# Layer 0 of a fused transformer kernel: modulation and the k and v sums by quarters of the features instead of halves, weights of v loaded later

## The chip, the cores and the metric

The kernel runs on one core of a Trainium2 chip. The metric is the device time in microseconds of one execution. The kernel before took 2399.53 us (median of three runs, 2398.6 to 2400.83). The execution that was profiled took 2408.4 us, of which 2406.5 us lie between its first and its last instruction (its span); times inside the kernel are counted from the start of that span.

## The reference, cut to what matters

The program is a stack of four attention-like layers on 256 latent and 256 context tokens of 1024 features, followed by a second block with a mixture of experts. Only the start of the first layer is changed:

```python
def modulation(cvec, w_ada, b_ada):
    return jnp.split(jax.nn.silu(cvec) @ w_ada + b_ada, 3, axis=-1)
...
        sh_l, sc_l, gt_l = modulation(c, w_ada, b_ada)
        sh_c, sc_c, gt_c = modulation(c_ctx, w_ada, b_ada)
        h_l = rmsnorm(x_lat, g_pre) * (1.0 + sc_l[:, None, :]) + sh_l[:, None, :]
        h_c = rmsnorm(x_ctx, g_pre) * (1.0 + sc_c) + sh_c
        y_l, y_c = mixer(h_l, h_c, need_ctx=need_ctx)
...
    q_l, k_l, v_l, z_l = jnp.split(h_lat @ w_in, cuts, axis=-1)
```

The shift `sh` and the scale `sc` are each 1024 numbers per condition vector; both come out of the first 2048 columns of `w_ada`, a matrix of 1024 x 3072 floats. Each of the 1024 features of `h` needs its own shift and scale, and k and v are sums over all 1024 features.

## The kernel before

Everything is float32. A product with weights is done in three passes on values that are split in a high and a low part (`two_parts`, L108: the high part on ACT, L110, the rest on DVE, L111; `wsplit`, L113, does it for a loaded weight tile; `mm3`, L124, issues the three products). The products of the modulation are plain float32, and the trace counts two MATMUL records for each of them.

When the kernel is built, a scheduler puts the instructions of the whole program in one list for each engine. Each engine runs its list in order and waits on semaphores where the list says so; the DMA queue that SP issues is such a list too. Loads of weights go through `load` (L100), which takes one of six buffers of 128 x 1024 floats (512 KB); a load can be issued when the buffer six loads back has been read.

Layer 0 starts in `first_layer` (L439), called by `layer_a` (L508):

- `tokens` (L445) loads and normalises four blocks of 128 tokens, transposes them on PE in eight batches of four (L452) and copies them to `xT`.
- The weights of v (`wv`, two loads, called by `w_v()`) are requested and split next, then the first half of the modulation, then the weights of k (`wk`, two loads).
- `modulation` (L456) works out shift and scale of one half of the features: eight loads of `l0_w_ada`, each 128 partitions with two pieces of 512 floats (shift and scale of eight rows of the matrix are spread over the partitions), and for each load two products of 32 rows x 512 columns. The four groups of 32 PSUM rows of the tile `ada` hold shift and scale of even loads (rows 0 to 63) and of odd loads (rows 64 to 127). The sum gets the bias (`plus`, L233 to L235), four transposes turn it (L469), and five small DVE instructions (L471 to L475) make the tiles `modB` (shift) and `modA` (scale).
- `modulated` (L477) applies them to the four blocks of 128 features of that half: half of the columns on DVE (L481), half on ACT (L482), then a split into `hT` (L110, L111).
- The loop over the two halves issues `modulated`, then the modulation of the other half, then for each block k of 128 features nine products of 128 x 256 for three of the four token blocks of v (PSUM tiles `s`, `s`, `o`) and six of 128 x 512 for k (PSUM tiles `mm`). The fourth token block of v (PSUM tile `t`, 24 products) comes last.

After that PE starts with the queries (`mm<-hT,wp`, 48 products for q and z of the first head pair), while DVE rotates the keys (`rope`, L427 to L432) and splits them; the first logits (`s<-ks,qs`) need the keys and the queries.

Of the kernel before, what the change touches and what calls it, by code (L numbers as in the profile page):

```python
# [9 lines left out]
F32 = mybir.dt.float32  # L10
# [4 lines left out]
ALU = mybir.AluOpType  # L15
# [36 lines left out]
def tile_model(ctx: ExitStack, tc: tile.TileContext, A, out):  # L52
    nc = tc.nc
    V, S, G, T = nc.vector, nc.scalar, nc.gpsimd, nc.tensor
# [5 lines left out]
    def right(name, bufs):  # L60
        return ph1.enter_context(tc.tile_pool(name=name, bufs=bufs, side="right"))
# [4 lines left out]
    tmp = right("tmp", 2)  # L66
# [13 lines left out]
    ident = cb[:, 0:128]  # L80
# [13 lines left out]
    def smc(name, i=0, n=None):  # L94
        o, w = SM[name]
        return sm[:, o + i:o + (w if n is None else i + n)]
# [3 lines left out]
    def load(src, shape):  # L100
        t = raw.tile([128, 1024], F32, name="w", tag="w")
        v = t[:, 0:int(np.prod(shape))]
        if len(shape) == 2:
            v = v.rearrange("p (a b) -> p a b", b=shape[1])
        loaded[0] = nc.sync.dma_start(v, src)
        return v

    def two_parts(hi, lo, src):  # L108

        S.activation(hi, src, AF.Copy)  # L110
        V.tensor_tensor(lo, src, hi, op=ALU.subtract)  # L111
# [18 lines left out]
    def psum(tag, shape=(512,), rows=128, bufs=None):  # L130
        if len(shape) == 1:
            return ps.tile([rows, shape[0]], F32, name=tag, tag=tag, bufs=bufs)
        return ps.tile([rows, *shape], F32, name=tag, tag=tag, bufs=bufs)

    def mm(o, l, r, start=True, stop=True):
        return T.matmul(o, l, r, start=start, stop=stop)  # L136

    def evac(o, i):

        cnt[0] += 1  # L140
        if cnt[0] % 2:
            S.activation(o, i, AF.Copy)
        else:
            V.tensor_copy(o, i)  # L144
# [13 lines left out]
    scT = cst1.tile([128, 2, 8, 32], F32, name="scT")  # L158
# [74 lines left out]
    def plus(p, brow, keep):  # L233
        m = mpool.tile([128, 512], F32, name="modg", tag="modg", bufs=2) if keep else tmp.tile([128, 512], F32, name="mod", tag="th")
        V.tensor_tensor(m, p, brow, op=ALU.add)  # L235
        return m

    def row(src):
        r = tmp.tile([128, 512], F32, name="rows", tag="rows", bufs=2)
        nc.sync.dma_start(r, src)  # L240
        return r
# [51 lines left out]
    def new_hT(n):  # L293

        hs = [hpool.tile([128, 4, 512], F32R, name="hT", tag="w") for _ in range(4 if n == 512 else 2)]
        if n == 256:
            return [[u[:, :, 256 * j:256 * j + 256] for u in hs] for j in range(2)]
        return hs[0:2], hs[2:4]
# [140 lines left out]
    def first_layer(lp, w_v, w_k):  # L439

        hT = new_hT(512)
        xT = [lp.tile([128, 2, 512], F32, name="xT", tag=tag, bufs=2) for tag in ("pT", "pT", "qs", "qs")]
        a, b = [mpool.tile([128, 8, 2], F32, name="mod" + c, tag="mod" + c, bufs=2) for c in "AB"]

        def tokens(t):  # L445
            nc.sync.dma_start(x[t], A["xin"][t])
            xn = normalised(t, hT)
            for hh in range(2):
                p = psum("t", (4, 128))
                for q in range(4):  # L450
                    k = hh * 4 + q
                    T.transpose(p[:, q, :], xn[:, k * 128:(k + 1) * 128], ident)  # L452
                for q in range(2):
                    evac(xT[2 * hh + q][:, :, t * 128:(t + 1) * 128], p[:, 2 * q:2 * q + 2])

        def modulation(hh):  # L456

            brow = row(A["rows0"][hh])
            p = psum("ada", bufs=1)
            wv = A["l0_w_ada"][:, 0:2048].rearrange("(p k) (b c) -> p k b c", k=8, b=2)  # L460
            for k in range(8):
                ch = load(wv[:, k, :, 512 * hh:512 * hh + 512], (2, 512))
                for j in range(2):
                    g = j + 2 * (k % 2)
                    mm(p[32 * g:32 * g + 32, :], scT[:, 0, k, :], ch[:, j, :], k < 2, k >= 6)
            m = plus(p, brow, False)
            p = psum("ada", (4, 128), bufs=1)
            for q in range(4):
                T.transpose(p[:, q, :], m[:, q * 128:(q + 1) * 128], ident)  # L469
            ks = slice(4 * hh, 4 * hh + 4)  # L470
            V.tensor_copy(b[:, ks], p[:, :, 0:2])  # L471
            V.tensor_tensor(b[:, ks], b[:, ks], p[:, :, 64:66], op=ALU.add)
            V.tensor_scalar(a[:, ks], p[:, :, 32:34], 1.0, None, ALU.add)
            V.tensor_tensor(a[:, ks], a[:, ks], p[:, :, 96:98], op=ALU.add)
            V.tensor_tensor(a[:, ks], a[:, ks], smc("gpre0")[:, ks].unsqueeze(2).to_broadcast([128, 4, 2]), op=ALU.mult)  # L475

        def modulated(hh):  # L477
            for k in range(4 * hh, 4 * hh + 4):
                f = tmp.tile([128, 512], F32, name="hf", tag="th")
                src = xT[k // 2][:, k % 2]  # L480
                V.tensor_scalar(f[:, 0:256], src[:, 0:256], a[:, k, 0:1], b[:, k, 0:1], ALU.mult, ALU.add)  # L481
                S.activation(f[:, 256:512], src[:, 256:512], AF.Identity, scale=a[:, k, 1:2], bias=b[:, k, 1:2])  # L482
                two_parts(hT[0][hh][:, k % 4], hT[1][hh][:, k % 4], f)

        for t in range(4):
            tokens(t)
        pv = [psum("s", (256,)), psum("s", (256,)), psum("o", (256,), bufs=1)]
        pk = [psum("mm") for _ in range(2)]
        wv = w_v()
        modulation(0)  # L490
        wk = w_k()
        for hh in range(2):
            modulated(hh)
            if not hh:
                modulation(1)
            for k in range(4 * hh, 4 * hh + 4):
                hk = [u[hh][:, k % 4] for u in hT]
                for t in range(3):
                    mm3(pv[t], [u[:, t * 128:(t + 1) * 128] for u in hk], [u[:, k % 4, :] for u in wv[hh]], k == 0, k == 7)
                for m in range(2):  # L500
                    mm3(pk[m], [u[:, k, :] for u in wk[m]], hk, k == 0, k == 7)
        pv.append(psum("t", (256,)))
        proj_t(pv[3], 3, wv, hT)
        begin_mods(0)
        begin_mods(1)
        return hT, pk, pv
# [1581 lines left out]
def _layout(inp):  # L2088
    f = np.float32
    inp = {k: np.asarray(v) for k, v in inp.items()}  # L2090
    d = dict(_consts())
# [37 lines left out]
    for i in range(4):  # L2129
        b = inp[f"l{i}_b_ada"].reshape(6, 512)  # L2130
# [8 lines left out]
    rows0 = np.zeros((2, 128, 512), f)  # L2139
# [2 lines left out]
            rows0[hh, [j, 32 + j]] = inp["l0_b_ada"].reshape(6, 512)[[hh, 2 + hh]]  # L2142
    d["rows0"] = rows0

    def blocks(w, width):

        n = w.shape[1] // width
        return np.ascontiguousarray(w.reshape(8, 128, n, width).transpose(2, 1, 0, 3))
# [36 lines left out]
    b = inp["b_ada_2"][0].reshape(12, 512)  # L2185
# [40 lines left out]
```

## Time and profile before

| | |
|---|---|
| median of three runs | 2399.53 us |
| the profiled execution | 2408.4 us |
| its span | 2406.5 us |
| PE busy in the span | 2226.5 us, 93% |
| DVE busy, ACT busy | 1188.2 us (49%), 725.9 us (30%) |
| mean granted TensorE clock | 0.96 of full speed |
| moved by DMA | 576.71 MB, 240 GB/s on average |

The profile is read in stages, because the shares are means over stages with different limits. The change lies in the first 70 us. Matmul records end when their pipeline is empty, so the time that a product takes among others is the distance of two starts, not the length of a record.

### The profile page before, as it was taken

To read this page: it belongs to the slowest core of one execution; us is meant where nothing else is said; L and a number is where in the kernel's file an instruction comes from. 1 tells how busy PE (TensorE), PEld (TensorE's weight loads), DVE (VectorE), ACT (ScalarE), POOL (GpSimd) and SP (SyncE) were. 2 spreads that over 40 slices of the span, in tenths; PEclk is the share of its full clock that TensorE was granted. 3 is DMA by queue.
4 is the path that set the end of the run, shared out by engine and by line. 5 is a ranking of instruction groups with operands and counts; after the bars stand their busy time and mean duration, and the time that the engine had idled before them with its cause. 6 is when DMAs were issued, how large, how long until landed. Compare 5 with 4: busy or idle time off the path is not lost. (4 is left out here: it accounts for less than half of the span.)

```text
span 2406.5 us, 32540 instructions
## 1 busy us (share of the span) xinstructions
PE 2226.5 (93%) x12516; PEld 1372.9 (57%) x12516; DVE 1188.2 (49%) x2545; ACT 725.9 (30%) x1588; POOL 79.8 (3%) x125
## 2 busy tenths in 40 slices
PE   7999999999999999998998899989989899999997
PEld 4767777777788887677864343333334333334342
DVE  3877666656666669867544123232323333322332
ACT  3555454345333456554232011010111110101101
POOL 0000010000000010002200000000000000000000
PEclk9999999999999999999999899999989989999998
DMA  8443432333333245646237978787999868999995
GB/s 305 132 149 127 136 119 78 98 125 125 115 102 122 80 127 180 206 162 249 80 111 305 371 312 351 281 350 278 413 414 415 333 257 354 378 413 413 413 377 230
DMA packets 124828, 576.71 MB, mean 240 GB/s; under 512 B 11953, under 2 KB 12721, under 8 KB 91762
## 3 DMA queue, kind: packets, MB, share of 16 engines
q1 hardware_dynamic: 124530, 572.71, 62.5%
q8 instruction: 190, 3.11, 0.5%
q14 instruction: 108, 0.88, 0.1%
HBM read 571.61 MB, written 1.05 MB: 238 GB/s over the span
## 5 line engine op out<-in xcount | busy, mean ns | idle before, releaser
L136 PE MATMUL hg<-w,xq 128*64 128x512 f32 x2048 | 500.2, 621 | 15.2 <-PEq L1899 6.7
L136 PE MATMUL mm<-hT,wp 128*128 128x256 f32 (+1 forms) x1776 | 351.2, 342 | 0.6 <-DVE aqk L144 0.5
L136 PEld LDWEIGHTS hg<-w,xq 128*64 128x64 f32 x2048 | 161.1, 143 | 323.3 <-issue 306.3
L136 PEld LDWEIGHTS mm<-hT,wp 128*128 128x128 f32 x1776 | 272.5, 190 | 54.2 <-issue 19.8
L1729 DVE TENSOR_SCALAR gm<-hg 128x512 f32<-128x512 f32 (+1 forms) x37 | 25.6, 691 | 436.2 <-PE hg L136 434.6
L1748 PE MATMUL py<-w,aT 128*64 128x512 f32 x992 | 221.3, 592 | 1.1 <-DMA w<-w 1.0
L111 DVE TENSOR_TENSOR wp<-w,wp 128x1024 fp32r<-128x1024 f32 (+2 forms) x149 | 178.7, 1204 | 75.5 <-ACT wp L110 72.1
L136 PE MATMUL mm<-wp,hT 128*128 128x256 f32 (+1 forms) x1584 | 198.1, 284 | 5.1 <-DVE mixT L419 3.0
L136 PEld LDWEIGHTS mm<-wp,hT 128*128 128x128 f32 x1584 | 191.0, 191 | 11.0 <-DVE mixT L419 3.2
L110 ACT ACTIVATE wp<-w 128x1024 fp32r<-128x1024 f32 (+2 forms) x149 | 153.8, 1035 | 101.3 <-PE mm L136 55.2
L1730 ACT ACTIVATE um<-gm 128x512 f32<-128x512 f32 x32 | 20.2, 630 | 528.8 <-DVE gm L1729 528.8
L1748 PEld LDWEIGHTS py<-w,aT 128*64 128x64 f32 x992 | 84.3, 137 | 131.0 <-issue 118.9
L110 ACT ACTIVATE yeh<-gm 64x512 fp32r<-64x512 f32 x62 | 39.0, 628 | 202.3 <-DVE gm L1872 202.1
L1872 DVE SCALAR_TENSOR_TENSOR gm<-py,gsq,g 64x512 f32<-64x512 f32 x62 | 46.5, 750 | 100.1 <-PE py L1748 99.1
L136 PE MATMUL ada<-w,scT 128*32 128x512 f32 x576 | 83.6, 625 | 5.8 <-DMA w<-l_w_ada 5.7
L136 PEld LDWEIGHTS g<-P,xc 128*128 128x128 f32 x496 | 57.8, 191 | 24.8 <-issue 24.8
L136 PE MATMUL g<-P,xc 128*128 128x128 f32 x496 | 63.8, 281 | 1.1 <-DVE P L1678 1.1
L136 PE MATMUL hg<-w,xs 128*32 128x512 f32 x480 | 60.0, 650 | 5.0 <-DVE xs L144 3.8
L136 PE MATMUL s<-wp,oz 128*128 128x512 f32 x264 | 64.1, 392 | 0.0
L1766 DVE TENSOR_TENSOR xl<-xl,py 128x512 f32<-128x512 f32 x60 | 39.7, 686 | 41.8 <-PE py L136 38.2
L136 PEld LDWEIGHTS s<-wp,oz 128*128 128x128 f32 x264 | 49.1, 188 | 13.3 <-issue 2.5
L587 ACT ACTIVATE e<-e,nm 128x512 f32<-128x512 f32 x64 | 45.7, 716 | 30.9 <-DVE nm L586 30.7
(606 smaller groups left out, 3039.6 us busy)
## 6 DMA issues: line engine op xcount, KB each, us to landing
w<-w SPq DMA_DIRECT2D x383, 1024.0 KB, 15.5
w<-l_w_ada SPq DMA_DIRECT2D x96, 512.0 KB, 4.3
w<-w_ada SPq DMA_DIRECT2D x48, 512.0 KB, 4.4
w<-l_w_z SPq DMA_DIRECT2D x32, 512.0 KB, 4.6
w<-l_w_out SPq DMA_DIRECT2D x32, 512.0 KB, 4.2
w<-l_w_q SPq DMA_DIRECT2D x16, 512.0 KB, 5.3
w<-l_w_v SPq DMA_DIRECT2D x12, 512.0 KB, 5.0
w<-w_dqkv SPq DMA_DIRECT2D x12, 512.0 KB, 4.4
```

Of the source, the lines that this page charges most:

```text
L110: S.activation(hi, src, AF.Copy)
L111: V.tensor_tensor(lo, src, hi, op=ALU.subtract)
L136: return T.matmul(o, l, r, start=start, stop=stop)
L587: S.activation(e, e, AF.Exp, scale=0.125, bias=nm[:, c:c + 1], accum_out=den[:, c:c + 1])
L1729: V.tensor_scalar(gm, gate, 7.0, None, ALU.min)
L1730: S.activation(um, gm, AF.Sigmoid, scale=1.702)
L1748: i = T.matmul(p[64 * hh:64 * hh + 64, :], aT[:, kk % 4, 64 * (kk // 4):64 * (kk // 4) + 64], w2_tile(e, kk, hh), start=kk == 0, stop=kk == 7)
L1766: V.tensor_tensor(y[:, t, sl], y[:, t, sl], py, op=ALU.add)
L1872: V.scalar_tensor_tensor(w, p, gs, g2, ALU.mult, ALU.mult)
```

## The change

The modulation is worked out in four quarters of 256 features instead of two halves of 512. A new array `l0_w_mod` holds the same 2048 columns of `l0_w_ada`, laid out by quarters so that a load of 512 KB brings 4 KB in one piece to each partition: shift and scale of two eighths of the contraction. There are four loads for a quarter, sixteen in all, as before. For each load there are now four products of 32 rows x 256 columns, one for each group of 32 PSUM rows. A quarter is turned by two transposes instead of four, and the five small DVE instructions run on half the columns, four times instead of twice. `modulated` runs over two feature blocks at a time, and the loop over k and v issues the next quarter after each. The weights of v are requested after the first quarter of the modulation instead of ahead of it. The old columns of `l0_w_ada` beyond 2048 are used as before.

```diff
@@ -453,29 +453,32 @@
                 for q in range(2):
                     evac(xT[2 * hh + q][:, :, t * 128:(t + 1) * 128], p[:, 2 * q:2 * q + 2])
 
-        def modulation(hh):
-
-            brow = row(A["rows0"][hh])
-            p = psum("ada", bufs=1)
-            wv = A["l0_w_ada"][:, 0:2048].rearrange("(p k) (b c) -> p k b c", k=8, b=2)
-            for k in range(8):
-                ch = load(wv[:, k, :, 512 * hh:512 * hh + 512], (2, 512))
-                for j in range(2):
-                    g = j + 2 * (k % 2)
-                    mm(p[32 * g:32 * g + 32, :], scT[:, 0, k, :], ch[:, j, :], k < 2, k >= 6)
-            m = plus(p, brow, False)
-            p = psum("ada", (4, 128), bufs=1)
-            for q in range(4):
-                T.transpose(p[:, q, :], m[:, q * 128:(q + 1) * 128], ident)
-            ks = slice(4 * hh, 4 * hh + 4)
+        brows = {}
+
+        def modulation(q):
+
+            if q % 2 == 0:
+                brows[q // 2] = row(A["rows0"][q // 2])
+            p = psum("ada", bufs=1)[:, 0:256]
+            for k in range(0, 8, 2):
+                ch = load(A["l0_w_mod"][q, :, 2 * k:2 * k + 4], (4, 256))
+                for g in range(4):
+                    mm(p[32 * g:32 * g + 32, :], scT[:, 0, k + g // 2, :], ch[:, g, :], k == 0, k == 6)
+            m = tmp.tile([128, 512], F32, name="mod", tag="th")[:, 0:256]
+            V.tensor_tensor(m, p, brows[q // 2][:, 256 * (q % 2):256 * (q % 2) + 256], op=ALU.add)
+            p = psum("ada", (4, 128), bufs=1)[:, 0:2]
+            for u in range(2):
+                T.transpose(p[:, u, :], m[:, u * 128:(u + 1) * 128], ident)
+            ks = slice(2 * q, 2 * q + 2)
             V.tensor_copy(b[:, ks], p[:, :, 0:2])
             V.tensor_tensor(b[:, ks], b[:, ks], p[:, :, 64:66], op=ALU.add)
             V.tensor_scalar(a[:, ks], p[:, :, 32:34], 1.0, None, ALU.add)
             V.tensor_tensor(a[:, ks], a[:, ks], p[:, :, 96:98], op=ALU.add)
-            V.tensor_tensor(a[:, ks], a[:, ks], smc("gpre0")[:, ks].unsqueeze(2).to_broadcast([128, 4, 2]), op=ALU.mult)
-
-        def modulated(hh):
-            for k in range(4 * hh, 4 * hh + 4):
+            V.tensor_tensor(a[:, ks], a[:, ks], smc("gpre0")[:, ks].unsqueeze(2).to_broadcast([128, 2, 2]), op=ALU.mult)
+
+        def modulated(q):
+            hh = q // 2
+            for k in (2 * q, 2 * q + 1):
                 f = tmp.tile([128, 512], F32, name="hf", tag="th")
                 src = xT[k // 2][:, k % 2]
                 V.tensor_scalar(f[:, 0:256], src[:, 0:256], a[:, k, 0:1], b[:, k, 0:1], ALU.mult, ALU.add)
@@ -486,14 +489,14 @@
             tokens(t)
         pv = [psum("s", (256,)), psum("s", (256,)), psum("o", (256,), bufs=1)]
         pk = [psum("mm") for _ in range(2)]
-        wv = w_v()
         modulation(0)
-        wk = w_k()
-        for hh in range(2):
-            modulated(hh)
-            if not hh:
-                modulation(1)
-            for k in range(4 * hh, 4 * hh + 4):
+        wv, wk = w_v(), w_k()
+        for part in range(4):
+            hh = part // 2
+            modulated(part)
+            if part < 3:
+                modulation(part + 1)
+            for k in (2 * part, 2 * part + 1):
                 hk = [u[hh][:, k % 4] for u in hT]
                 for t in range(3):
                     mm3(pv[t], [u[:, t * 128:(t + 1) * 128] for u in hk], [u[:, k % 4, :] for u in wv[hh]], k == 0, k == 7)
@@ -2142,6 +2145,8 @@
             rows0[hh, [j, 32 + j]] = inp["l0_b_ada"].reshape(6, 512)[[hh, 2 + hh]]
     d["rows0"] = rows0
 
+    d["l0_w_mod"] = inp["l0_w_ada"][:, 0:2048].reshape(128, 8, 2, 4, 256).transpose(3, 0, 1, 2, 4).reshape(4, 128, 16, 256)
+
     def blocks(w, width):
 
         n = w.shape[1] // width
```

What the scheduler makes of it differs from before on SP, PE, DVE and ACT up to the first logits of layer 0; from there on each engine has the same instructions in the same order.

SP, the list of transfers from the first tokens to the tables after the modulation. `xl` and `xc` are the tokens, `w` is the ring of six weight buffers. Before:

```order
L446 DMA xl<-xin 128x1024 x2
L446 DMA xc<-xin 128x1024 x2
L105 DMA w<-l_w_v 128x1024 x2
L240 DMA rows<-rows 128x512
L105 DMA w<-l_w_ada 128x2x512 x8
L105 DMA w<-l_w_k 128x1024 x2
L240 DMA rows<-rows 128x512
L105 DMA w<-l_w_ada 128x2x512 x8
```

Now:

```order
L446 DMA xl<-xin 128x1024 x2
L446 DMA xc<-xin 128x1024 x2
L240 DMA rows<-rows 128x512
L105 DMA w<-l_w_mod 128x1024 x4
L105 DMA w<-l_w_v 128x1024 x2
L105 DMA w<-l_w_k 128x1024 x2
L105 DMA w<-l_w_mod 128x1024 x4
L240 DMA rows<-rows 128x512
L105 DMA w<-l_w_mod 128x1024 x8
```

Four loads of the modulation now stand ahead of the weights of v and k, and twelve behind them; before, eight stood between v and k.

DVE, from the last of the five small instructions of the first part of the modulation to the bias of the next part. `hf` is the modulated block, `hT` its low part, `wv` and `wp` the low parts of the weights of v and of k. Before:

```order
L475 TENSOR_TENSOR modA<-modA,sm 128x8
L481 TENSOR_SCALAR hf<-xT,modA,modB 128x256
L111 TENSOR_TENSOR wp<-w,wp 128x1024
L481 TENSOR_SCALAR hf<-xT,modA,modB 128x256
L111 TENSOR_TENSOR wp<-w,wp 128x1024
L111 TENSOR_TENSOR hT<-hf,hT 128x512 x2
L481 TENSOR_SCALAR hf<-xT,modA,modB 128x256 x2
L111 TENSOR_TENSOR hT<-hf,hT 128x512 x2
L235 TENSOR_TENSOR mod<-ada,rows 128x512
```

Now:

```order
L477 TENSOR_TENSOR modA<-modA,sm 128x4
L484 TENSOR_SCALAR hf<-xT,modA,modB 128x256
L111 TENSOR_TENSOR wv<-w,wv 128x1024
L484 TENSOR_SCALAR hf<-xT,modA,modB 128x256
L111 TENSOR_TENSOR wv<-w,wv 128x1024
L111 TENSOR_TENSOR hT<-hf,hT 128x512
L111 TENSOR_TENSOR wp<-w,wp 128x1024
L111 TENSOR_TENSOR hT<-hf,hT 128x512
L111 TENSOR_TENSOR wp<-w,wp 128x1024
L468 TENSOR_TENSOR mod<-ada,rows 128x256
```

The splits of the weights of v moved from the transposes of the tokens to here, so four weight splits instead of two stand between the first modulated blocks and the next part of the modulation.

PE, around the second part of the modulation. `ada` with `w` are the products of the modulation, `ada` with `mod` its transposes; `s`, `o` and `t` are the sums of v, `mm` those of k. Before:

```order
L136 MATMUL ada<-w,scT 32x512 x2
L136 MATMUL mm<-hT,wp 128x512 x4
L469 MATMUL ada<-cb,mod 128x128 x4
L136 MATMUL s<-wv,hT 128x256 x6
L136 MATMUL o<-wv,hT 128x256 x3
L136 MATMUL mm<-hT,wp 128x512 x6
L136 MATMUL t<-wv,hT 128x256 x3
```

Now, after the second of four parts:

```order
L136 MATMUL mm<-hT,wp 128x512 x5
L136 MATMUL ada<-w,scT 32x256 x4
L136 MATMUL mm<-hT,wp 128x512
L136 MATMUL t<-wv,hT 128x256 x4
L471 MATMUL ada<-cb,mod 128x128 x2
L136 MATMUL t<-wv,hT 128x256 x2
L136 MATMUL ada<-w,scT 32x256 x8
L136 MATMUL s<-wv,hT 128x256 x4
```

Behind the transposes PE now has two products of v and two loads' worth of the next part before it needs the modulated blocks of this part; before, it had a whole block of 15 products and three of `t`.

## Rows read from the trace of the kernel before

**Rows 1.** The page, busy us, share of the span and instructions by engine:

```profile
PE 2226.5 (93%) x12516; PEld 1372.9 (57%) x12516; DVE 1188.2 (49%) x2545; ACT 725.9 (30%) x1588; POOL 79.8 (3%) x125
```

**Rows 2.** Windows: from:to, length, busy per engine (instructions), clock, DMA share, GB/s:

```profile
27.00:32.40 5.40, 1.12 (x4) 0.72 (x4) 3.79 (x10) 3.65 (x6) 0.00 (x0) 0.50 1.03 387
32.40:37.00 4.60, 4.58 (x20) 2.37 (x22) 3.85 (x7) 2.73 (x5) 0.00 (x0) 0.59 1.02 353
37.00:49.00 12.00, 12.00 (x56) 5.38 (x53) 0.09 (x1) 0.00 (x0) 0.00 (x0) 1.00 0.69 260
49.00:65.20 16.20, 16.20 (x107) 14.66 (x107) 8.80 (x22) 8.61 (x16) 0.00 (x0) 1.00 0.50 180
```

**Rows 3.** Timeline of PE, 9 to 27 us: start, length, what, idle and releaser:

```profile
9.17 3.22 PE L452 MATMUL t<-cb,xn 128*128 128x128 f32 x12 [9.17 <-DVE xn L308]
16.14 1.92 PE L136 MATMUL ada<-w,scT 128*32 128x512 f32 x2
...
20.03 0.66 PE L452 MATMUL t<-cb,xn 128*128 128x128 f32 x4
20.62 1.92 PE L136 MATMUL ada<-w,scT 128*32 128x512 f32 x16
...
25.45 1.49 PE L136 MATMUL ada<-w,scT 128*32 128x512 f32 x4 [0.27 <-DMA w<-l_w_ada]
```

**Rows 4.** Timeline of ACT, the first split of a weight of v:

```profile
11.54 1.05 ACT L110 ACTIVATE wv<-w 128x1024 fp32r<-128x1024 f32 x1
```

**Rows 5.** Timeline of all engines, from the first half's bias to the first product:

```profile
26.97 0.69 DVE L235 TENSOR_TENSOR mod<-ada,rows 128x512 f32<-128x512 f32 x1 [5.41 <-PE ada L136]
...
27.72 1.12 PE L469 MATMUL ada<-cb,mod 128*128 128x128 f32 x4 [0.79 <-DVE mod L235]
...
29.81 1.09 ACT L482 ACTIVATE hf<-xT,modB,modA 128x256 f32<-128x256 f32 x2 [1.35 <-DVE modA L475]
30.07 1.22 DVE L111 TENSOR_TENSOR wp<-w,wp 128x1024 fp32r<-128x1024 f32 x1
...
32.42 0.80 PE L136 MATMUL s<-wv,hT 128*128 128x256 f32 x2 [3.58 <-ACT hT L110]
33.02 1.29 DVE L111 TENSOR_TENSOR hT<-hf,hT 128x512 fp32r<-128x512 f32 x2
```

**Rows 6.** Timeline of PE, products of the modulation among those of k and v:

```profile
33.15 1.94 PE L136 MATMUL ada<-w,scT 128*32 128x512 f32 x8
...
41.25 1.05 PE L136 MATMUL ada<-w,scT 128*32 128x512 f32 x4
42.23 0.39 PE L136 MATMUL o<-wv,hT 128*128 128x256 f32 x1
...
56.69 1.54 PE L136 MATMUL mm<-hT,wp 128*128 128x512 f32 x6
...
59.10 1.54 PE L136 MATMUL mm<-hT,wp 128*128 128x512 f32 x6
...
62.90 2.57 PE L136 MATMUL t<-wv,hT 128*128 128x256 f32 x21
```

**Rows 7.** Timeline of PE, second half: its transposes, and the first product behind them:

```profile
49.83 0.60 PE L469 MATMUL ada<-cb,mod 128*128 128x128 f32 x4
...
53.08 0.74 PE L136 MATMUL s<-wv,hT 128*128 128x256 f32 x4
```

**Rows 8.** Timeline of DVE and PE, from the keys to the first logits:

```profile
63.04 0.28 DVE L427 COPY ropeb<-kT 32x256 f32<-32x256 f32 x1 [1.23 <-ACT kT L142]
...
79.10 1.41 DVE L569 TENSOR_TENSOR qs<-qT,qs 64x512 fp32r<-64x512 f32 x2
79.84 1.20 PE L136 MATMUL s<-ks,qs 128*128 128x512 f32 x4 [0.87 <-DVE qs L569]
```

**Rows 9.** Windows of PE, two single microseconds: length, busy, clock, DMA share, GB/s:

```profile
26.00:27.00 1.00, 0.93 (x4) 0.50 1.09 401
...
36.00:37.00 1.00, 1.00 (x8) 0.92 0.99 279
```

## The prediction

> **What bounds the kernel now.** The page first: PE is busy 93% of the span [rows 1], so what counts is where PE waits. The windows by stage put the waits of the first 70 us ahead of 32.4 us: between 27 and 32.4 us PE works 1.12 us of 5.4, and from 37 us on it has no idle time up to 65.2 us [rows 2]. The timeline gives the cause: PE's last product of the first half of the modulation waits for its load and ends at 25.45 + 1.49 = 26.94 us [rows 3]; bias, four transposes, five small DVE steps, the modulated block and its split follow one by one, and the first product of v starts at 32.42 us [rows 5]. The transfers run at 387 GB/s meanwhile [rows 2], and ten loads of 512 KB (two for v, eight for the modulation) stand ahead of that point. So the stage has two parts: until 32.42 us a chain of loads and small steps ends last, after it PE itself.
>
> The sum is made against the profiled execution, 2408.4 us; the median of the runs is 2399.53 us, 8.9 us less, and I carry the difference found over to the median.
>
> **The change, part by part.**
>
> *First quarter of the modulation.* Four loads are enough now, and they take the places of the loads for v. The first of those had landed by 11.54 us [rows 4]; with the 256 KB of `rows` ahead and 0.524 MB / 387 GB/s = 1.35 us for each load, the fourth lands at about 16 us. PE isn't ready for it. Its list has 32 transposes and 16 products of the modulation, interleaved. [...] A lone 512-column product takes 1.92 us there [rows 3], one of 256 columns thus about 1.0 us. From 12.4 us (9.17 + 3.22): 1.0 for one product, 2.15 for eight transposes, 2 x 1.0 for the rest of load 1 and for load 2, 2.15 for eight transposes: 19.7 us. Then at full pace four pieces of about 0.5: the last product ends at 21.7 us, 5.2 us ahead of 26.94.
>
> How early the pace doubles is open. [...]
>
> *From there to the first product of v.* Before: 32.42 - 26.97 = 5.45 us [rows 5]. The bias has half the columns (0.69 us becomes about 0.42, an estimate from that row), two transposes instead of four (1.12 us becomes 0.56 at the lower pace); the small steps are bound by their start and stay. ACT splits one weight of v between the blocks where it split one of k. So 5.45 - 0.83 = 4.6, and the first product stands at 26.3 us, 6.1 us ahead.
>
> *What PE has to do from there until the sums of k are done* (62.90 us, where the last 21 products of `t` start [rows 6]). Before, 62.90 - 32.42 = 30.5 us:
> - eight blocks of nine and six products, one every 59.10 - 56.69 = 2.42 us: 19.4;
> - modulation [rows 6]: 1.9 us for the pair of loads at 33.15, six single loads at 42.23 - 41.25 = 0.98 plus about 0.2 for changing over (an estimate: the `o` product behind one has a record of 0.39 us, where the 21 of `t` stand 2.41 / 21 = 0.115 apart): 9.0 in all;
> - transposes 0.36, three products of `t` 0.35.
>
> That is 29.1; the other 1.4 us are the lower clock, 0.50 from 26 us until it rises in the 37th microsecond [rows 9], after 3 us of steady products.
>
> After:
> - the same 19.4, and 7 products of `t` (four move ahead of the end): 0.8;
> - twelve loads of the modulation in ten places. No row shows a 256-column product. From below: sixteen records (eight products, four loads) took 1.92 us when four groups of rows overlapped [rows 3], 0.48 us for two loads' groups at half the columns. From above: if the groups don't overlap better than the two of a single load did, 0.98. I take 0.55, nearest to the lower row, because now all four groups come with one load: 12 x 0.55 + 10 x 0.2 = 8.6;
> - three times two transposes: 1.05.
>
> Sum 29.85. To it come waits that weren't there:
> - *DVE in the first quarter.* Four weight splits of 1.22 us [rows 5] instead of two stand among the first blocks, because those of v left the stage of the transposes. The first modulated block stood 29.81 - 26.97 = 2.84 us behind the bias [rows 5], now 0.83 less: 21.7 + 2.0 = 23.7. From there DVE has block, split of v, block, then a wait for ACT (two blocks 1.09 [rows 5], second split 1.05 [rows 4]: until 25.9); then 1.2 + 0.65 + 1.2 + 0.65 + 1.2 = 30.8 us. Until then PE has 2.42 + 0.75 = 3.2 us of work, begun at 26.3, so it loses 30.8 - 29.5 = 1.3.
> - *The second quarter.* From the end of the transposes to the product that uses them: 53.08 - 50.43 = 2.65 us [rows 7]. PE has two products of `t` and two loads behind them, 0.25 + 1.3: it waits 1.1. In quarters three and four a block stands between (2.9 to 3.3 us of work): nothing.
> - *The lower clock.* Up to 30.8 us it is covered by DVE; beyond that between 0 and 1.4 us as before. I take 0.7.
>
> Together 29.85 + 3.1 = 33.0, so the sums of k are done at 59.3 us instead of 62.9: 3.6 us ahead.
>
> *Loads.* Six buffers now hold the weights of v and k until DVE has split them, so loads 7 to 11 of the modulation start only at 25 to 31 us. Three of them one behind the other take 3 x 1.35 = 4.1 us, and by the list above PE asks for each 3 to 8 us after it is free to start. I cost that at nothing: PE's own work on the blocks hides it, and if DVE fell 4 us behind, every further us would show. The loads of q and z queue behind these; the queries need them only after the sums. POOL's list isn't touched.
>
> *After the sums.* DVE is the bound from the first rotated key at 63.04 us to the split queries at 79.10, where PE waits 0.87 us for it [rows 8]. It does the same steps in that stretch, so the logits come ahead by what the sums of k came ahead; the four products of `t` that moved (0.46 us) are lost in that wait. From there the lists agree, so the gain stays: **3.5 us**, 2396.0 us by the median. That is 0.15%, inside the 0.2% (4.8 us) that a measurement of this kernel can tell from no change.
>
> **The rivals.**
>
> *The clock rises earlier at the start.* [...] Then three to four pieces of about 1.0 run in 0.5 each, the chain to the keys starts 1.7 us earlier, and PE keeps 1.1 to 2.2 us of that, as DVE's splits shift with it. Against: the early products are short and stand among transposes. It gives 2396.0 - 1.6 = 2394.4 us. Chance 0.2.
>
> *The clock stays low longer.* PE's start is spotty now: 1.3 us of waits by 30.8 us, 1.1 us in the second quarter. If it runs at 0.50 until 36 us as before, 5.2 us do the work of 2.6: 1.9 us more than I counted. If the waits of the second quarter let it fall once more, 1.5 more. 2398 to 2399.4 us. For: before, it was down from 26 us on [rows 9], after PE had waited for loads between short products. Against: from 30.8 us on PE is about as busy as it was before the rise at 36 us. Chance 0.23.
>
> *Four groups don't overlap (slower).* If a load costs 0.98 as a single load did [rows 6], twelve loads cost 12 x 0.43 = 5.2 us more, and the four at the start about 2.3 us: 3.5 turns into -4.0, 2403.5 us. It turns from gain to loss where a load costs 0.55 + 3.5/16 = 0.77 us. Against: the sixteen records in 1.92 us. Chance 0.07.
>
> **How the numbers follow.** The forecast, with 1.5 us to either side for the terms that I estimated, has 0.5. The range takes in the two clocks and reaches from 2391.8 to 2400.4 us: it leaves out most of the slower rival and about 0.1 at the fast end, where an early clock and short loads (0.48) come together. Faster by over 0.2% (below 2394.7 us): most of the early clock and the forecast's fast edge, 0.27. Slower by over 0.2% needs the third rival with the low clock as well: 0.04. Within: 0.69.
>
> **What would show it.** The last product of the first quarter near 21.7 us; first product of v near 26.3; on DVE four splits in a row up to 30.8 with PE waiting for them; starts of a load's products 0.5 to 0.6 us apart; an idle time of about 1 us ahead of the third pair of blocks; the queries starting near 59.3 + 17 x 0.115 = 61.3 us; the wait ahead of the first logits grown by 0.5 us. It is wrong if a load takes over 0.77 us, if the clock is low beyond 33 us, or if a later stage doesn't shift with the logits.

## The result and the profile after

The changed kernel takes 2373.63 us (median of 6 runs, 2365.69 to 2376.36), the kernel before 2400.34 us in the runs beside it (6 runs, 2398.6 to 2407.28). The ratio is 0.9879, 95% interval [0.9858, 0.9899]: about 27 us less, where 3.5 were forecast. The profiled execution takes 2374.81 us, with a span of 2373.0. That of before, at 2408.4 us, lies some 10 us over the medians of its kernel (2394.5 to 2400.3 in all comparisons here), so the two traces differ by 33.5 us, and not each difference between them is the change's.

The page's line of the engines, after (it answers [rows 1]):

```profile
PE 2209.1 (93%) x12580; PEld 1363.3 (57%) x12580; DVE 1189.4 (50%) x2557; ACT 726.2 (31%) x1588; POOL 80.3 (3%) x125
```

PE is busy 17.4 us less although it has 64 products more, and idle 16 us less (2373.0 - 2209.1 = 163.9 against 180.0). Where that lies is read stage by stage. First the stage that was changed: the timeline of PE after, to be laid beside [rows 3, 5, 6, 8]. Columns: start, length in us, what, and in brackets the idle time before it with its releaser.

```profile
9.03 3.23 PE L452 MATMUL t<-cb,xn 128*128 128x128 f32 x12 [9.03 <-DVE xn L308]
12.18 1.06 PE L136 MATMUL ada<-w,scT 128*32 128x256 f32 x2
13.17 1.93 PE L452 MATMUL t<-cb,xn 128*128 128x128 f32 x8
15.03 1.06 PE L136 MATMUL ada<-w,scT 128*32 128x256 f32 x14
16.03 1.09 PE L452 MATMUL t<-cb,xn 128*128 128x128 f32 x8
...
18.20 1.06 PE L136 MATMUL ada<-w,scT 128*32 128x256 f32 x14
...
23.81 1.22 PE L136 MATMUL s<-wv,hT 128*128 128x256 f32 x4 [3.56 <-ACT hT L110]
...
29.47 0.64 PE L136 MATMUL ada<-w,scT 128*32 128x256 f32 x8
30.04 0.97 PE L136 MATMUL s<-wv,hT 128*128 128x256 f32 x6
...
57.48 2.17 PE L136 MATMUL t<-wv,hT 128*128 128x256 f32 x17
59.49 11.36 PE L136 MATMUL mm<-hT,wp 128*128 128x512 f32 x48
...
74.34 1.18 PE L136 MATMUL s<-ks,qs 128*128 128x512 f32 x4 [1.20 <-DVE qs L572]
```

The first quarter is done at 18.20 + 1.06 = 19.26 us (before: the first half at 26.94), the first product of v starts at 23.81 instead of 32.42, the sums of k are done at 57.48 instead of 62.90, and the logits start at 74.34 instead of 79.84: 5.5 us ahead. Until here the change does what it says, 2 us better than forecast.

The rest comes much later. Between the first logits and some 115 us (times of before) a few instructions of the first layer's attention still stand in another order than before, so the lists agree later than the section on the change says. From there on PE, DVE, ACT and POOL run the same instructions in the same order. I matched DVE's instructions of the two traces one by one: the lead is 5.5 us at the first logits, 6.6 at 175 us, 11 at 1475, 32 at 1975. It grows most where the experts are worked out one after the other. Each expert copies its gate once to `gsq`; that copy serves as a mark. The answer for its line in the stretch of 1470 to 2010 us, before and after (count, shortest/median/longest ns, then the first and the last start):

```profile
L1707 DVE COPY gsq<-g x8: 150/150/150, 1491.4 to 2006.4; 128x2 f32<-128x2 f32 x8
```

```profile
L1710 DVE COPY gsq<-g x8: 150/150/152, 1480.3 to 1973.2; 128x2 f32<-128x2 f32 x8
```

In both it is the copies of the 4th to the 11th expert. The same seven experts take 515.0 us before and 492.9 us after: 22 us, in a stage that the diff doesn't touch. I call this the **expert stretch** below.

What PE waits for there, from 1000 us to the end (total, times, longest, us), first before, then after:

```profile
PE hg L136 <- PEq L1885: 10.2, 6, 6.2
PE hg L136 <- PEq L1899: 6.7, 10, 5.2
PE g L1739 <- PEq L1899: 5.5, 1, 5.5
...
PE hg L136 <- issue: 4.0, 3, 3.1
```

```profile
PE hg L136 <- PEq L1902: 6.5, 10, 5.0
PE g L1742 <- PEq L1902: 5.2, 1, 5.2
PE g L136 <- PEq L1888: 4.8, 1, 4.8
```

PEq is PE's own sequencer, and L1885 and L1899 (L1888 and L1902 after) are the two `tc.If(n > 64, ...)` around the work of an expert that more than 64 tokens chose. All rows of PEq and of issue together are 39.8 us before and 24.4 after; the largest waits for DVE and ACT are the same to 0.1 us (`gsq` 19.0, `yeh` 16.7). So the largest waits for data are not what changed. One such place in the timeline of PE, the end of the same expert, before:

```profile
1883.62 0.39 PE L136 MATMUL py<-yel,gTq 128*128 128x512 f32 x1
1885.37 0.50 PE L136 MATMUL py<-yeh,gTq 128*128 128x512 f32 x1 [1.36 <-ACT yeh L110]
1892.08 1.06 PE L136 MATMUL hg<-b1p,sel 96*64 96x512 bf16 x4 [6.21 <-PEq L1885]
```

and after:

```profile
1863.39 0.51 PE L136 MATMUL py<-yeh,gTq 128*128 128x512 f32 x1 [1.35 <-ACT yeh L110]
1864.04 0.62 PE L136 MATMUL hg<-b1p,sel 96*64 96x512 bf16 x4
1864.59 0.51 PE L136 MATMUL py<-yel,gTq 128*128 128x512 f32 x1
```

The same product waits 6.21 us before and not at all after. During that wait of before the DMA queues (1885.4 to 1892 us; packets, MB, share) show

```profile
q1 hardware_dynamic: 548, 2.69, 101.5%
q8 instruction: 1, 0.02, 1.0%
q14 instruction: 1, 0.01, 0.3%
```

a transfer of the instruction queue of 0.02 MB, while the weights of the experts fill the engines. In the whole trace this queue carries 190 such packets, 3.11 MB, so 16.4 KB each; I take them for code that comes in blocks. Between 100 and 1000 us, ahead of the experts, there are 42, one for some 251 of the 10561 products and weight loads that PE has there (after: 42, one for some 255 of 10697). One packet proves little, since in the expert stretch of before one comes every 9 us (58 in 515 us). But each of the eight waits of over 2 us on PEq or issue that PE has behind 1000 us in the trace of before holds one, inside it or in flight at its start.

### The profile page after: what moved, and what is told of

The parts are those of the page before. It is cut to its first block, busy times and chain, and to the rows that moved or that the text cites. A ratio compares the mean times of both kernels' runs of the same rounds, so it can differ in the third digit from the quotient of the medians.

```text
span 2373.0 us, 32692 instructions
## 1 busy us (share of the span) xinstructions
PE 2209.1 (93%) x12580; PEld 1363.3 (57%) x12580; DVE 1189.4 (50%) x2557; ACT 726.2 (31%) x1588; POOL 80.3 (3%) x125
## 5 line engine op out<-in xcount | busy, mean ns | idle before, releaser
L136 PE MATMUL hg<-w,xq 128*64 128x512 f32 x2048 | 492.5, 615 | 13.2 <-PEq L1902 6.5
L136 PE MATMUL ada<-w,scT 128*32 128x512 f32 (+1 forms) x640 | 79.2, 574 | 4.9 <-DMA w<-l_w_ada 3.9
L111 DVE TENSOR_TENSOR yel<-gm,yeh 64x512 fp32r<-64x512 f32 x60 | 41.2, 687 | 26.3 <-ACT yeh L110 25.4
## 6 DMA issues: line engine op xcount, KB each, us to landing
w<-w SPq DMA_DIRECT2D x383, 1024.0 KB, 16.4
```

## The experiments

Three theories. **A, position in time:** a lead of 5 us shifts where PE's gaps fall, and with them the spells at the lower clock. **B, carry:** later stages are lastingly faster by themselves, so a delay costs just itself. **C, place of the code:** the change makes PE's program longer by 130 instructions (64 products, 64 weight loads, 2 semaphore waits, counted in the traces) in front of everything later, so the ends of the code blocks fall elsewhere against the branches of the experts. Medians are compared within a job; before took 2394.48 us in the first, 2395.51 in the second, 2397.54 in the third.

**A delay of some 5.7 us, in the changed kernel and in the one before.** Both repeat the last products of v:

```
-        proj_t(pv[3], 3, wv, hT)
+        for r in range(3):
+            proj_t(pv[3], 3, wv, hT)
```

> The changed kernel, but the 24 products of the fourth token block of v are worked out three times (the first two results are thrown away). That adds 48 x 0.115 = 5.5 us to PE between the sums of k and the queries, of which up to 1.2 us go into the wait ahead of the first logits: the logits should stand at 78.6 to 79.9 us, within about 1 us of where they stand in the kernel before (79.84), and 4.3 to 5.5 us behind the changed kernel (74.34). Theory A, the gain behind the first layer hangs on where PE's idle gaps fall in time, and with that on the spells at the lower clock: the later work stands again where it stood before, so most of the 22 us are lost again, and the time lies at 2390 to 2405 us. Theory B, something in the changed kernel makes the later stages faster for good, whatever the hour: the delay is all that is added, 2373.6 + 4.3 to 5.5 = 2378 to 2379 us.

> The kernel before, with the same 48 products more at the same place: 5.5 us on PE, 0.9 us of them hidden by the wait ahead of the first logits, so the logits at 84 to 85 us. Theory A: the spells at the lower clock change their places, and the time moves by something else than the delay: below 2400 or above 2410 us. Theory B: 2400.3 + 4.6 = 2405 us, within 2 us.

e1: 2397.22 us, ratio 1.001 [0.9987, 1.0032], all of the gain gone. e2: 2388.57 us, ratio 0.998 [0.9958, 1.0001]: B's 4.6 us more lie outside that interval, which reaches from 10 us less to 0.2 us more. B falls with both. A stood, but explained nothing in advance: its bound for e2 (below 2400 us) holds for the kernel before in this job as well. The first product of the logits moved less than expected, to 76.50 us in e1 and 81.98 in e2, but at 175 us the whole delay is there (6.4 us in both, by the table below). Seen from C, each of these edits also adds 96 instructions to PE.

**The change's two parts.** e3 moves only the loads of v's weights behind the first modulation, by halves as before; e4 has the quarters, with v's weights loaded first as before.

```
-        wv = w_v()
         modulation(0)
-        wk = w_k()
+        wv, wk = w_v(), w_k()
```

```
+        wv = w_v()
         modulation(0)
-        wv, wk = w_v(), w_k()
+        wk = w_k()
```

(the second against the changed kernel)

> The kernel before, with nothing of the change but the place of the weights of v: their loads and splits stand behind the first half of the modulation (halves, old layout). The first half's last load comes two loads (2.7 us) sooner, but four splits of 1.22 us stand between the first blocks, so the sums of k should be done within 2 us of 62.9. Theory A: the time moves by more than the sums of k do, either way, by up to 20 us. Theory B, if the later gain comes from the order of the loads of v: it shows here, 2375 to 2382 us; if not, 2398 to 2402 us.

> The changed kernel, with the weights of v loaded and split ahead of the modulation as in the kernel before. The fourth load of the modulation comes two loads later than in the changed kernel, but only two splits stand between the first blocks: the first product of v at 25 to 27 us, the sums of k done at 57 to 60 us (62.9 before, 57.5 with the whole change). Theory A: the time is anywhere between 2365 and 2405 us, by the spells, and doesn't follow from the sums of k. Theory B, if the later gain comes from the quarters: 2373 to 2377 us.

e3: 2397.81 us, ratio 1.0008 [0.9985, 1.0031]; e4: 2376.72 us, 0.9909 [0.988, 0.9938]. The quarters carry the effect or most of it (18 us against the kernel before in this job, where the whole change has some 26 in others), the later loads alone none. In e4's trace the logits start at 73.08 us, sooner than with the whole change; in e3's at 81.19. PE's program is 2 instructions shorter in e3 and 130 longer in e4: this doesn't separate A from C.

**Only the code is moved.** PE has nothing to do until 9 us. There, ahead of the first transpose, stand products of one element on constants that are set at once:

```
     V.memset(scT, 0.0)
+    pz = psum("t", (4, 128))
+    for _ in range(32):
+        mm(pz[0:1, 0, 0:1], mhalf[:, 0:1], mhalf[:, 0:1])
```

e5 has them in the kernel before (128 instructions), e6 in the changed kernel (258 in all), e8 has 40 of them in e1's kernel (386), and e7 is the changed kernel once more.

> The kernel before with 32 products of a single element ahead of the first transpose, where TensorE waits for the first rows until 9.17 us anyway. No other work is moved in time; only TensorE's program gets longer by about as many instructions as the change adds to it (64 products and their 64 weight loads). Theory A (the gain behind the first layer hangs on where the work falls in time, by way of the clock): first logits and total unchanged, 2392 to 2397 us, and TensorE's waits on its own sequencer, on issue and on the branches of the expert stage (from 1000 us on) stay near 37 us. Theory C (the gain behind the first layer comes from where the boundaries of the code blocks that the instruction queue brings in fall against the branches of the expert stage): those waits fall to about 24 us as in the changed kernel, and the total is 2378 to 2384 us although the first layer gains nothing.

> The changed kernel with the same 32 products of one element at the start: TensorE's program is now some 258 instructions longer than before's, about one block of the instruction queue (16 KB), so that the block boundaries of the expert stage lie as in the kernel before. Theory A: 2372 to 2377 us, as the changed kernel, waits near 24 us. Theory C: the waits of the expert stage come back to about 37 us, and the total is 2386 to 2391 us: only the 5.5 us of the first layer and a little of the clock are left of the gain.

> The changed kernel itself, beside the others on one chip, and for a second profile of it. Both theories: 2371 to 2377 us; the logits 5 to 6 us sooner than before, and waits of the expert stage near 24 us again, at the same branches as in its first profile.

> The changed kernel with the delay of e1_after_delay (the last products of v three times) and 40 products of one element at the start, which bring TensorE's program from 226 to some 386 instructions over before's, that is one block more than the changed kernel's 130. Theory A: 2395 to 2399 us, as e1_after_delay, since the work falls at the same times. Theory C: the code lies as in the changed kernel, waits near 24 us, and the total is the changed kernel's and the delay of 5.7 us: 2376 to 2383 us.

In the trace of e5 they cost nothing, since the rows come later anyway:

```profile
0.92 1.74 PE L136 MATMUL t<-mhalf 128*1 128x1 f32 x64 [0.92 <-DVE mhalf L92]
9.11 3.23 PE L455 MATMUL t<-cb,xn 128*128 128x128 f32 x12 [6.45 <-DVE xn L311]
```

e5: 2386.31 us, ratio 0.9955 [0.9932, 0.9978], without any earlier logits worth naming (0.8 us). e6: 2396.78 us, 1.0002 [0.9977, 1.0026]: the changed kernel loses its gain to 32 products that nobody waits for. e7: 2369.84 us, 0.9899 [0.9865, 0.9934], 1 us under its range; its logits start at 75.00 us, 4.8 us ahead of before where the first profile has 5.5. e8: 2376.04 us, 0.991 [0.9879, 0.9942]: e1's kernel with 40 products more is 19.5 us below before, where e1 was 2.7 above. A says that e8 equals e1, e6 equals e7 and e5 equals before; it is wrong three times. In e5, PE, DVE and ACT run the instructions of before behind the new products in the same order, and in e6 those of the changed kernel (but for one pair on DVE), so that only the place of PE's code is different. The first and last mark of the expert stretch, in e6 and in e8:

```profile
L1713 DVE COPY gsq<-g x8: 148/148/150, 1476.0 to 1995.8; 128x2 f32<-128x2 f32 x8
```

```profile
L1714 DVE COPY gsq<-g x8: 147/148/149, 1485.6 to 1980.1; 128x2 f32<-128x2 f32 x8
```

519.8 us in e6, as before (515.0), and 494.5 in e8, as after. e6's program is 258 instructions longer than before's, e8's is 256 longer than the changed kernel's. Of e6's waits of over 2 us in the stretch, these are back, the last of them at the product shown above:

```profile
1521.40 0.39 PE L136 MATMUL py<-yeh,gTq 128*128 128x512 f32 x1 [3.43 <-issue]
...
1884.89 1.06 PE L136 MATMUL hg<-b1p,sel 96*64 96x512 bf16 x4 [5.71 <-PEq L1891]
```

C had the sign and the place, not each size: e6 lies 6 us over its range, e5 2 us, and e5's waits are 30.4 us, not 24.

**The changed kernel's place exactly, and other places.** e9 is e5 with one bf16 product more (two instructions, 130 in all); e10, e11 and e12 are the changed kernel with 16, 24 and 48 of the products of one element.

```
+    mbf = const.tile([128, 16], BF16, name="mbf")
+    V.memset(mbf, -0.5)
...
     for _ in range(32):
         mm(pz[0:1, 0, 0:1], mhalf[:, 0:1], mhalf[:, 0:1])
+    mm(pz[0:1, 0, 0:1], mbf[:, 0:1], mbf[:, 0:1])
```

> e5_before_shift with one more product (its weight load and its matrix instruction), so that TensorE's program of the kernel before is longer by 130 instructions, exactly as far as the changed kernel's, where e5's was by 128. Theory C (the places of the code blocks against the branches decide the gain behind the first layer): the stall of some 5 us between 1880 and 1900 us that e5 kept goes too, waits near 24 us, total 2375 to 2381 us, the changed kernel's and its 5 us in the first layer. A rival in which e5's missing part has nothing to do with the code: 2384 to 2389 us, as e5.

> The changed kernel with 16 products of one element at the start: TensorE's program 194 instructions over before's instead of 130, a quarter of a block on. Theory C: another set of stalls at the branches, so a total that may lie anywhere from the changed kernel's 2372 to 2391 us, and waits of the expert stage that go with it (each us of waits at least one us of time). Without an influence of the code: 2371 to 2377 us.

> The changed kernel with 24 products of one element at the start: 226 instructions over before's, the code layout of e1_after_delay without its delay of 5.7 us. Theory C: waits near 34 us at the same branches as in e1, total 2387 to 2394 us, that is e1's 2397 less the delay. Theory A (it was the delay that cost 24 us in e1): 2371 to 2377 us.

> The changed kernel with 48 products of one element at the start: 322 instructions over before's, 66 past a whole block. Theory C: not the changed kernel's layout, so again a total between 2372 and 2392 us with waits of the expert stage that go with it. Without an influence of the code: 2371 to 2377 us.

e9: 2377.2 us, ratio 0.992 [0.9899, 0.9941]. The kernel before, with its halves and its logits at the old time, has most of the changed kernel's gain, through 33 products that compute nothing. Its marks:

```profile
L1713 DVE COPY gsq<-g x8: 148/150/150, 1484.3 to 1978.9; 128x2 f32<-128x2 f32 x8
```

494.6 us, with no wait of over 2 us in the stretch. (The one that e5 kept there isn't at the product named above, as the expectation has it: it is 2.41 us on issue, at 1802 us.) The rival's 2384 to 2389 us are out. e10: 2379.37 us, 0.9935 [0.9911, 0.996]; e11: 2388.91 us, 0.9966 [0.9947, 0.9985], 8.6 below before in its job, where e1 was 2.7 above before in its own: 11 us apart where the delay is 5.7, and its waits are 39.0 us instead of 34; e12: 2394.34 us, 0.9991 [0.9971, 1.001], 2 us over its range.

All kernels in the order of their place in a block, which I take as 256 instructions (an estimate from the 251 and 255 above, and from e6 and e8): PE's instructions over before's; what is left of that after taking off 256; the expert stretch of the profiled run and all waits for PEq and issue from 1000 us on; the logits' region against before (median of DVE's instructions between 175 and 200 us); the time.

| kernel | longer by | place | stretch, us | waits, us | at 175 us | median, us |
|---|---|---|---|---|---|---|
| e1 | 226 | 226 | 503.6 | 33.5 | -0.2 | 2397.2 |
| e11 | 226 | 226 | 511.3 | 39.0 | -5.8 | 2388.9 |
| e3 | -2 | 254 | 511.5 | 38.5 | +0.2 | 2397.8 |
| before | 0 | 0 | 515.0 | 39.8 | 0 | 2394.5 to 2400.3 |
| e6 | 258 | 2 | 519.8 | 39.5 | -3.6 | 2396.8 |
| e12 | 322 | 66 | 510.5 | 37.1 | -4.6 | 2394.3 |
| e2 | 96 | 96 | 492.4 | 25.4 | +6.4 | 2388.6 |
| e5 | 128 | 128 | 496.3 | 30.4 | -1.4 | 2386.3 |
| e9 | 130 | 130 | 494.6 | 23.3 | +0.4 | 2377.2 |
| e8 | 386 | 130 | 494.5 | 24.2 | -1.1 | 2376.0 |
| e4 | 130 | 130 | 497.9 | 26.1 | -7.2 | 2376.7 |
| after, e7 | 130 | 130 | 492.9, 494.5 | 24.4, 23.1 | -6.6, -4.2 | 2373.6, 2369.8 |
| e10 | 194 | 194 | 504.7 | 33.9 | -7.2 | 2379.4 |

The five profiled runs at place 130 agree in stretch and waits whatever their first layer does; those around 0 agree as well. With 256 to 258 instructions more the stretch is nearly the same again: 515.0 us before and 519.8 in e6, 492.9 after and 494.5 in e8. Stretch and waits are each those of one execution, which for before lies 8 to 14 us above the median of its kernel, for e3 and e11 9 us. Nor do waits and medians go together one to one: e1 waits 6 us less than before and is no faster. What the traces and runs show is this: packets of 16.4 KB on the instruction queue, about one for 251 to 255 of PE's products and weight loads where no expert stands, a stretch that comes back after some 256 instructions, and waits of up to 6.21 us behind the `If`s. That such a wait is one for code is theory C's reading of these; no row shows it by itself.

## Why the prediction was wrong

**The step that failed is the last:** "From there the lists agree, so the gain stays". The lists do agree, from 115 us on, and the first layer's lead is still there at 175 us. But equal lists aren't equal programs: the same instructions lie 130 further on in PE's code, and the later stages moved by far more than the logits, where the prediction had them move together. Of some 26 us, e9 gives the part of the place alone: 2397.5 - 2377.2 = 20 us. The other 5 or so fit the 4.8 and 5.5 us by which the logits came sooner in the two traces of the changed kernel. Its ratio is 0.988 to 0.990 where e9's is 0.992, and e8, without most of the lead, takes 6.2 us more than e7 beside it (2376.0 and 2369.8). These differences are no larger than the intervals, so the medians alone don't show that part. The change makes the programs of DVE and ACT a little longer too (12 instructions more on DVE); no run moves those by themselves. That the four groups of a quarter add 32 products, each recorded as two, to PE's program was in front of me as a cost of 8.6 us and not as a length.

What the 20 us consist of can be read from the expert stretch, 515.0 us before and 494.6 in e9. PE's windows over it, from the first mark to the last, before and then e9 (length, busy with the count of products, clock, DMA share, GB/s):

```profile
1491.40:2006.40 515.00, 464.49 (x2444) 0.94 0.86 344
```

```profile
1484.30:1978.90 494.60, 457.08 (x2444) 0.97 0.88 359
```

PE runs the same 2444 products. In e9 it idles 13.0 us less (37.5 against 50.5), and its waits for PEq and issue there are 12.8 us less (5.8 against 18.6). It is busy 7.4 us less, at a granted clock of 0.97 instead of 0.94. The lower clock goes with the waits: the windows around the two longest waits of before in the stretch, and around the same products in e9, show

```profile
1783.00:1795.00 12.00, 8.90 (x27) 0.57 1.03 408
1885.00:1897.00 12.00, 5.42 (x12) 0.57 1.03 412
```

```profile
1770.80:1782.80 12.00, 12.00 (x53) 0.89 1.03 421
1867.20:1879.20 12.00, 11.43 (x42) 0.86 1.02 423
```

so PE loses the wait itself and works at the lower level around it (the clock records of before show 0.50 from 1783.8 to 1794.0 and from 1886.2 to 1896.4 us). Nothing else is left over: in all 14 profiled kernels PE's busy time in the stretch, less half of its part at the lower level, comes to 440 to 442 us (worked out from the clock records of the traces), so that idle time and clock are the whole difference between them there.

Over whole executions time and clock go together too: over all 30 runs of before in the first job the correlation of time and mean granted clock is -0.89, and the means of the runs are 0.965 to 0.966 for before, 0.970 for the changed kernel (6 runs), 0.971 for e9. But not every spell at the lower clock belongs to the place: that of before between 350 and 400 us (0.90 there, 1.00 after) is missing or shorter in every other profiled kernel, with the gain or without. Open is how two instructions of place make up e5's 9 us over e9: their stretches differ by 1.7 us, their waits by 7.1, and 3 of these lie behind the stretch.

Now the steps of the first layer.

- *The first quarter ends at 21.7 us.* It ended at 19.26, 2.4 us sooner. The rival of the early clock came true: twelve transposes at 9.03 us take 3.23 us and eight at 13.17 take 1.93, but the eight at 16.03, after the first products at 12.18 and 15.03, take 1.09. Before, the pace rose only behind the product at 16.14 [rows 3]: four transposes took 1.12 us at 17.99 and 0.66 at 20.03. For the slow part no run shows a level of the clock: the records of the granted clock begin at 14.9 us after and at 19.1 before, both with 1.00, about where the pace rises. The forecast's steps up to 19.7 us thus carry on the pace of [rows 3], and the four pieces of about 0.5 us at full pace behind them were my estimate; at 18.20 us 14 records of 256 columns took 1.06 us. The first record stands 2.7 us (after) and 3.0 us (before) behind the start of the first product of the modulation; two traces make no rule.
- *First product of v 4.6 us behind the bias.* 23.81 - 19.32 = 4.5: right, and so it stood 2.5 us ahead of the forecast.
- *PE waits 1.3 us for DVE's four splits.* Wrong. They stand at 21.46, 23.27, 25.01 and 26.75 us, the last done at 27.97, and PE has no wait between 23.81 and 35 us. The products of the next quarter's loads filled it, and at the lower clock PE's own work was longer. The windows after (length, busy of PE, PEld, DVE, ACT, POOL with counts, clock, DMA share, GB/s):

```profile
20.00:27.00 7.00, 3.44 (x13) 2.50 (x12) 6.31 (x13) 4.98 (x7) 0.00 (x0) 0.63 0.79 247
27.00:32.40 5.40, 5.40 (x40) 2.99 (x40) 0.97 (x1) 0.00 (x0) 0.00 (x0) 0.85 0.91 328
```

- *The lower clock beyond that, 0.7 us.* Too little, in return. The granted clock is 0.63 from 20 to 27 us, and its 0.85 from 27 to 32.4 us means (1 - 0.85) x 5.4 / 0.5 = 1.6 us at the lower level (0.50), so that it rose for good at some 28.6 us. PE's first 4.8 us behind 23.81 thus did the work of 2.4. The two errors nearly cancel: from the first product of v to the sums of k it was 57.48 - 23.81 = 33.7 us, where 33.0 were forecast.
- *0.55 us for a load's products.* 30.04 - 29.47 = 0.57: right, and the slower rival, which needed 0.77, is out.
- *1.1 us of waiting in the second quarter.* 0.78 us on the modulated block, and 0.52 us on issue a little ahead of it: right.
- *Loads cost nothing.* Right: from 19 to 60 us PE waits for no DMA.
- *Queries at 61.3 us, the wait ahead of the logits grown by 0.5.* 59.49, and 1.20 us against 0.87: the queries came with the quarter's 2 us, the wait grew by 0.33. DVE's chain shifted along as forecast.

So the first layer gave 5.5 us (4.8 in the second profile) in place of 3.5, and the term that was mis-sized is the pace at the start. The rival that had it gave 2394.4 us. No case that I wrote down held the 20 us.

## What to carry to other kernels

In a kernel with branches an edit changes one more number, the length of each engine's program ahead of them; here, for PE's, the same stretch took 492.4 to 519.8 us. After an edit, look for waits on the engine's own sequencer and on issue behind the branches, and compare kernels with the program padded to the same place (a few products of one element in a gap that is there anyway) before the edit is credited with the difference. Here the padded kernel before (2377 us) shows that some 20 of the 26 us are not the change's own; what is left for it, about 5 us, is no larger than the intervals. The padding, which cost nothing in an idle gap (1.74 us of work ahead of 9.11 us in e5), is worth a try of its own. A gain that appears far behind the edit, in a stage that the diff doesn't touch, is no carry until a kernel without the edit has been seen without it.

## What the runs showed of the hardware

- Behind an `If` PE waited up to 6.21 us on its own sequencer, with one 16.4 KB packet of the instruction queue inside the wait and the weights at 101.5% of the DMA engines (rows above). The same stretch of seven experts takes 492.4 to 519.8 us, by the place of the same instructions in the code. The effect repeats when PE's program grows by some 256 instructions (before 515.0 us and e6 519.8, after 492.9 and e8 494.5).
- Such a wait came with a lower clock as well: around the two longest in the expert stretch of before the granted clock was 0.57, around the same products without the wait 0.86 to 0.89.
- A place isn't just good or bad: between 96 and 130 the stretch is 492 to 498 us, at 194 it is 504.7, at 226 up to 511.3, at 254 to 2 it is 511.5 to 519.8, and at 66 still 510.5. From place to place the waits of over 2 us stand at other products (at 1521, 1780 and 1885 us in e6, at 1826 and 1948 us in e10), and all waits for PEq and issue come to 39.5 us in the one and 33.9 in the other. Two waits of 4.4 to 5.7 us, between 1305 and 1370 us behind the second `If`, are there in all 14 profiled kernels: no place tried here removes them.
- 64 recorded products of one element took 1.74 us, 27 ns each. With their weight loads they are 128 instructions, half of the 256 after which the stretch repeats, so filling that much costs less than 2 us (an estimate from that row) even where no idle time hides it.
